# A hybrid diffusion step: the third modulation set of layers 1 to 3 summed on VectorE

## Chip, cores and metric

The kernel runs on one core of one Trainium2 chip. The metric is device time in microseconds (us); lower is better. The kernel before was timed three times, and one more execution of it was profiled; all stretches below are counted from the start of that execution's span.

## What is computed

One inference step through four layers on 384 tokens of width 1024 (128 context tokens, 256 latent tokens). Layer l mixes tokens by l mod 3: 0 is a bidirectional Mamba-2 scan (SSD), 1 a short gated convolution, 2 differential attention. So the order is SSD, short convolution, attention, SSD. Every layer then has a gated convolutional feed-forward net (FFN).

```python
mod = silu(cond) @ w_mod[l] + b_mod[l]            # cond: c_ctx for context tokens, c for latent ones
sh1, sc1, gt1, sh2, sc2, gt2 = split(mod, 6)      # six rows of 1024
m = mixer(rmsnorm(x, g[0]) * (1 + sc1) + sh1)
x = x + gt1 * rmsnorm(m, g[1])
f = ffn(rmsnorm(x, g[2]) * (1 + sc2) + sh2)       # (silu(gate) * val) @ w_down, after a 3-tap conv of h @ w_up
x = x + gt2 * rmsnorm(f, g[3])
```

The change concerns the first line: a product of two condition rows (context and latent) with a 1024 x 6144 float32 matrix per layer, 25 MB of weights.

## The kernel before

**Products.** Activations lie transposed, 128 channels on the partitions and 384 tokens along the free axis. All weights come as float32; each chunk of 128x1024 is loaded into `wr`, copied by ACT (ScalarE) to a rounded `wh` (line 155), and DVE (VectorE) writes the rest `wl = wr - wh` (line 156). A product is three matmuls, `wh*hh`, `wh*hl` and `wl*hh` (line 340 for channel-major results, line 380 for token-major ones, line 811 for the attention projections). `ahead` (line 143) keeps four chunks split (WS = 4) and three more loaded (WR = 4 buffers) ahead of the chunk that PE (TensorE) works on.

**Up products.** `ffn` (line 462) has 22 blocks. A block takes two chunks and two PSUM banks of five, 48 matmuls of 128x384. Then `conv` takes each of its two halves through one ACT copy (line 396) and four DVE operations (lines 398 and 400, two each), ACT does the SiLU (line 475) and DVE the product into `g[i]` (line 476). The down product follows in `tm_out`; its `prep` splits `g[k]` into `gh` and `gl` (lines 405 and 406).

**Modulation.** The 6144 columns of a layer are three sets s = 0, 1, 2 of 2048, and each set eight units, one for each block kb of 128 input channels. `mod_units` (line 167) makes for each unit a load of 1 MB (tag `wm` with one buffer, or `wx` with `room` buffers of the running stage's pool) and four float32 matmuls (line 187) of a stationary 128x32 (`sil`, the two condition columns and 30 zero columns) with 512 moving columns, placed in four column strips of the array, so that they can run beside each other. The profile shows each of the four as two instructions, so a unit is eight instructions of line 187. The eight units of a set add up in one PSUM bank; `mod_finish` (line 195) adds the bias row, multiplies by the norm weight (lines 197 and 198), turns the result with four PE transposes into `cm`, and writes the gates of sets 1 and 2 to memory (`gd`), from where `gates` broadcasts them. Set 0 is needed before a layer's mixer, set 1 at the end of the mixer, set 2 for the middle norm and the FFN's gate.

**Where the units run.** All 96 units stand in one list, `filler`. `pace` (line 242) takes units from it so that after each phase of a layer a given count is done: the numbers in `PACE` are the counts for the end of the mixer's products, the middle turn (mixer's out product and norm), the up products, and the end turn. Layer n = 0 does its own sets 1 and 2 in its mixer (16 units) and then 13 units of layer 1. A later mixer has 11 units: the last three of its set 1, and set 2. `need` takes units that are still missing when a set is used. `stock` loads ahead as many units as there are buffers.

**Order.** All loads are issued by one queue, SP's, in order. The order of instructions on each engine is made when the kernel is built: the framework keeps the program's order as a priority and lets later instructions go ahead on a simulated timeline where an engine would be idle. [...]

Of the kernel before, what the change touches and what calls it, by code (L numbers as in the profile page):

```python
# [10 lines left out]
F32 = mybir.dt.float32  # L11
# [8 lines left out]
P = 128  # L20
# [19 lines left out]
HB = 2  # L40
PACE = (24, 31, 32, 37)
CB = 9


class Net:
# [29 lines left out]
    def consts(self):  # L75
# [12 lines left out]
        self.V.memset(self.brow, 0.0)  # L88
        self.S.activation(self.sil, self.sil, AF.Silu)

    def consts2(self):
# [75 lines left out]
    def mod_units(self, l):  # L167
# [24 lines left out]

        return [(lambda s=s, kb=kb: load(s, kb), lambda raw, s=s, kb=kb: unit(s, kb, raw)) for s in range(3) for kb in range(KB)]

# [47 lines left out]
    def pace(self, phase, n, of):  # L242

        lo, hi = self.goal[phase]
        self.fill(lo + (hi - lo) * n // of - (24 * len(self.layers) - len(self.filler)))

# [104 lines left out]
    def tm_out(self, *args, room, **kw):  # L351

        with self.tc.tile_pool(name="out", bufs=1, reuse_waits="tile") as self.op:
            self.room, self.hbufs = room, HB
            self.stock()
            self._tm_out(*args, **kw)
            self.room = 0

    def _tm_out(self, l, gate, nk, prep, eps=None, then=None):
# [49 lines left out]
    def run(self):  # L409
# [6 lines left out]
        for l in self.layers:  # L416
            self.filler += self.mod_units(l)
        l0 = self.layers[0]
        with tc.tile_pool(name="in", bufs=1, reuse_waits="tile") as self.op, self.banked(mm=5):
# [14 lines left out]
        for n, l in enumerate(self.layers):  # L434
            nxt = self.layers[n + 1] if n + 1 < len(self.layers) else None
            marks = [8 if n == 0 else 24 * n + 16] + [24 * n + m for m in PACE]
            self.goal = dict(zip(("mix", "mid", "ffn", "end"), zip(marks, marks[1:])))
# [21 lines left out]
            with tc.tile_pool(name=f"ffn{l}", bufs=1, reuse_waits="tile") as pl, self.banked(mm=5):  # L459
                self.ffn(l, pl, end)  # L460

    def ffn(self, l, pl, then):
        d = self.d
# [3 lines left out]
        with self.tc.tile_pool(name=f"up{l}", bufs=1, reuse_waits="tile") as self.cpool:  # L467
            self.cbufs = 7
            for i in range(NF):
                ch = self.cm_weights(2)  # L470
                pg = self.cm_block(ch, 2, 0)
# [4 lines left out]
                self.V.tensor_tensor(g[i], tg, tv, op=ALU.mult)  # L476
                self.pace("ffn", i + 1, NF)

        def prep(k):
# [544 lines left out]
```

## Time and profile before

| | |
|---|---|
| median of 3 runs | 2422.38 us (2415.94 to 2424.57) |
| the profiled execution, own time | 2417.66 us |
| its span, first to last instruction | 2415.9 us |
| PE busy in the span | 2295.4 us (95%) |
| DVE busy | 1621.2 us (67%) |
| ACT busy | 1253.4 us (52%) |
| mean granted TensorE clock | 0.977 of full speed |
| moved by DMA | 391.79 MB |

The stages in the span: SSD mixer of layer 0 until about 448, its up products to 637, down products and end turn to 744; layer 1 (short convolution) to 912, up products to 1095, down to 1202; layer 2 (attention) to 1451, up products to 1637, down to 1745; layer 3 (SSD) to 2132, up products to 2317, down to the end. PE is matmul, PEld weight load, SPq SP's queue. A matmul's shown duration overlaps with the next one's, so what a matmul costs is read from the distance of the starts, and the sums of durations exceed the time. Releasers of waits are inferred.

### The profile page before, as it was taken

How to read it: one execution, taken by the hardware profiler on the slowest of the kernel's cores; microseconds unless marked ns; L12 is line 12 of the kernel's file. 1: busy time of each engine (PE TensorE's matmuls, PEld its weight loads, DVE VectorE, ACT ScalarE, POOL GpSimd, SP SyncE). 2: the span in 40 equal slices, each digit the busy share in tenths (PEclk: the TensorE clock that was granted, in tenths of full speed). 3: DMA queues.
4: the chain of work that ended last, by engine and by line, in shares of the span. 5: the costliest groups of instructions: out<-in, count | busy, mean ns of one | idle time of the engine just before them, and what ended most of it. 6: DMA issues, size and time to landing. Idle time of an engine off the chain costs nothing.

```text
span 2415.9 us, 35621 instructions
## 1 busy us (share of the span) xinstructions
PE 2295.4 (95%) x13132; PEld 2002.2 (83%) x13132; DVE 1621.2 (67%) x2930; ACT 1253.4 (52%) x2173; POOL 334.2 (14%) x498
## 2 busy tenths in 40 slices
PE   6989999899999999999999979999998999989998
PEld 3878887699987969998688649998687888779987
DVE  3787876577655457776655547776578888677765
ACT  3666765444444344444544444444556776554444
POOL 1122330100001010000123320000113323010000
PEclk7999999999999999999999999999999999989999
DMA  7556655533537564335435463335455654423442
GB/s 286 181 162 207 202 192 177 201 132 122 166 111 288 204 245 138 125 122 166 155 106 176 155 244 107 123 127 162 147 159 171 200 159 153 139 97 123 131 146 81
DMA packets 113374, 391.79 MB, mean 162 GB/s; under 512 B 13104, under 2 KB 25520, under 8 KB 100912
## 3 DMA queue, kind: packets, MB, share of 16 engines
q1 hardware_dynamic: 113200, 389.52, 49.2%
q8 instruction: 103, 1.69, 0.3%
q14 instruction: 71, 0.58, 0.1%
HBM read 382.39 MB, written 7.08 MB: 161 GB/s over the span
## 4 chain that ended last, share of the span: by engine, by line
PE 78%; DVE 9%; DMA 6%; ACT 3%; issue 2%; POOL 2%; SPq 0%; POOLq 0%; ACTq 0%; DVEq 0%
PE mm L340 44%; PE mm L380 20%; PE mm L811 4%; DMA wm<-in_w_mod 3%; PE modps L187 2%; PE yp L380 2%; DVE e L686 2%; DVE wl L156 1%; PE yp L726 1%; DVE w L690 1%; PE yp L852 1%; ACT jk L263 1%; DVE cv L398 1%; DMA wx<-in_w_mod 1%; PE yp L340 1%
## 5 line engine op out<-in xcount | busy, mean ns | idle before, releaser
L340 PE MATMUL mm<-hh,wh 128*128 128x384 f32 (+1 forms) x2352 | 796.4, 340 | 14.9 <-DVE cv L400 9.8
L340 PE MATMUL mm<-hl,wh 128*128 128x384 f32 (+1 forms) x2352 | 793.8, 338 | 0.0
L340 PE MATMUL mm<-hh,wl 128*128 128x384 f32 (+1 forms) x2352 | 792.0, 338 | 0.0
L156 DVE TENSOR_TENSOR wl<-wr,wh 128x1024 fp32r<-128x1024 f32 (+2 forms) x466 | 564.4, 1213 | 259.7 <-ACT wh L155 257.6
L155 ACT ACTIVATE wh<-wr 128x1024 fp32r<-128x1024 f32 (+2 forms) x466 | 483.3, 1039 | 313.1 <-PE mm L340 243.9
L340 PEld LDWEIGHTS mm<-hh,wh 128*128 128x128 f32 (+1 forms) x2352 | 443.3, 189 | 38.9 <-DVE cv L400 14.6
L340 PEld LDWEIGHTS mm<-hh,wl 128*128 128x128 f32 (+1 forms) x2352 | 442.3, 188 | 5.3 <-issue 3.4
L340 PEld LDWEIGHTS mm<-hl,wh 128*128 128x128 f32 (+1 forms) x2352 | 442.6, 188 | 4.5 <-issue 2.2
L396 ACT ACTIVATE cv<-mm,fcw 128x384 f32<-128x384 f32 x176 | 100.1, 571 | 233.4 <-PE mm L340 228.2
L380 PE MATMUL mm<-wh,gh 128*128 128x512 f32 x528 | 208.7, 395 | 0.0
L380 PE MATMUL mm<-wl,gh 128*128 128x512 f32 x528 | 208.6, 395 | 0.0
L380 PE MATMUL mm<-wh,gl 128*128 128x512 f32 x528 | 207.9, 395 | 0.0
L271 POOL TENSOR_SCALAR m<-s 128x1 f32<-128x1 f32 x42 | 17.2, 409 | 1145.5 <-ACT jk L263 1144.7
L398 DVE SCALAR_TENSOR_TENSOR cv<-mm,fcw,cv 128x127 f32<-128x127 f32 x352 | 144.1, 410 | 42.6 <-ACT cv L396 42.6
L405 ACT ACTIVATE gh<-fg 128x384 fp32r<-128x384 f32 x176 | 92.2, 524 | 152.6 <-PE mm L380 151.7
L406 DVE TENSOR_TENSOR gl<-fg,gh 128x384 fp32r<-128x384 f32 x176 | 97.6, 557 | 96.7 <-ACT gh L405 96.1
L400 DVE SCALAR_TENSOR_TENSOR cv<-mm,fcw,cv 128x127 f32<-128x127 f32 x352 | 145.8, 415 | 10.8
L380 PEld LDWEIGHTS mm<-wh,gh 128*128 128x128 f32 x528 | 99.0, 187 | 25.0 <-issue 0.8
L380 PEld LDWEIGHTS mm<-wh,gl 128*128 128x128 f32 x528 | 99.0, 187 | 24.2
L380 PEld LDWEIGHTS mm<-wl,gh 128*128 128x128 f32 x528 | 99.0, 187 | 23.9
L187 PE MATMUL modps<-wm,sil 128*32 128x512 f32 x496 | 78.3, 655 | 18.5 <-DMA wm<-in_w_mod 17.6
L683 POOL TENSOR_TENSOR w<-cb,dt 128x512 f32<-128x512 f32 x48 | 71.6, 1504 | 92.5 <-DVE w L691 91.6
(224 smaller groups left out, 3180.9 us busy)
## 6 DMA issues: line engine op xcount, KB each, us to landing
wr<-in_ffn_up SPq DMA_DIRECT2D x176, 512.0 KB
wm<-in_w_mod SPq DMA_DIRECT2D x62, 1024.0 KB
wr<-in_ssd_in SPq DMA_DIRECT2D x96, 512.0 KB
wr<-in_ffn_down SPq DMA_DIRECT2D x88, 512.0 KB
wx<-in_w_mod SPq DMA_DIRECT2D x34, 1024.0 KB
ab<-acs SPq DMA_DIRECT2D x48, 512.0 KB
wr<-in_ssd_out SPq DMA_DIRECT2D x32, 512.0 KB
wr<-in_sc_in SPq DMA_DIRECT2D x32, 384.0 KB
```

Of the source, the lines that this page charges most:

```text
L155: self.S.activation(hi[:, :m], raw[:, :m], AF.Copy)
L156: self.V.tensor_tensor(lo[:, :m], raw[:, :m], hi[:, :m].bitcast(F32), op=ALU.subtract)
L187: self.PE.matmul(acc[32 * j:32 * j + 32, :], self.sil[:, kb, :], raws[:, j // 2, (j % 2) * 512:(j % 2 + 1) * 512], start=kb == 0, stop=kb ...
L340: self.PE.matmul(acc[:m], w, h, start=n == 0, stop=n == len(ops) - 1)
L380: self.PE.matmul(acc[t], g[:, o:o + n], w, start=k == 0 and i == 0, stop=k == nk - 1 and i == 2)
L396: self.S.activation(t, src, AF.Copy, scale=cw[:, 1:2])
L398: self.V.scalar_tensor_tensor(t[:, o + 1:o + n], src[:, o:o + n - 1], cw[:, 0:1], t[:, o + 1:o + n], op0=ALU.mult, op1=ALU.add)
L400: self.V.scalar_tensor_tensor(t[:, o:o + n - 1], src[:, o + 1:o + n], cw[:, 2:3], t[:, o:o + n - 1], op0=ALU.mult, op1=ALU.add)
L405: self.S.activation(hi, src, AF.Copy)
L406: self.V.tensor_sub(lo, src, hi.bitcast(F32))
L683: GP.tensor_tensor(h4(w), cb[:, 1, t, None, :].to_broadcast([P, 4, P]), per(dt, 1), op=ALU.mult)
L811: PE.matmul(acc[t][:, :256], h[k][:, o:o + m], w[:, ws], start=k == 0 and i == 0, stop=k == KB - 1 and i == 2)
```

## The change

Sets 0 and 1 stay as they are, and so do all three sets of layer 0. Set 2 of layers 1, 2 and 3 leaves the list (`filler` has 24 + 3 x 16 = 72 units). It is computed beside the up products of the layer before. `mod_sums` goes through the eight channel blocks in halves of 1024 columns, 16 steps. A step loads 512 KB (`wv`, two buffers) and does two DVE operations on 128x1024, one for each condition row: `acc = raw * sil + acc`, with `sil` as a scalar on each partition. Sixteen of the 22 up blocks have such a step ahead of their own work (those with i mod 4 not 3, until the steps are used up). After the last block `mod_total` adds the 128 partitions on PE, with a stationary 128x32 that has ones in column c: four column strips for each of the two condition rows, eight matmuls, in the shape of two units. Then `mod_finish` runs as before.

`PACE` is moved by the eight units that each later layer lacks. `pace` also limits how many units `stock` loads ahead to those still due in the phase, and `tm_out` loads the next unit at its end, after its pool's room is set to 0.

```diff
-PACE = (24, 31, 32, 37)
+PACE = (0, 7, 8, 13)
...
+        self.onec = cp.tile([P, 2, 32], F32, name="onec")
+        self.V.memset(self.onec, 0.0)
+        for c in range(2):
+            self.V.memset(self.onec[:, c, c:c + 1], 1.0)
...
-        return [(lambda s=s, kb=kb: load(s, kb), lambda raw, s=s, kb=kb: unit(s, kb, raw)) for s in range(3) for kb in range(KB)]
+        sets = range(3 if l == self.layers[0] else 2)
+        return [(lambda s=s, kb=kb: load(s, kb), lambda raw, s=s, kb=kb: unit(s, kb, raw)) for s in sets for kb in range(KB)]
+
+    def mod_sums(self, l, s, pool):
+        acc = pool.tile([P, 2, 2048], F32, name="macc")
+        for kb in range(KB):
+            for hf in range(2):
+                raw = pool.tile([P, 1024], F32, tag="wv", name="wv", bufs=2)
+                self.load(raw, self.d["w_mod"][l, s, kb][:, hf])
+                for c in range(2):
+                    a, w = acc[:, c, hf * 1024:(hf + 1) * 1024], self.sil[:, kb, c:c + 1]
+                    if kb == 0:
+                        self.V.tensor_scalar(a, raw, w, None, op0=ALU.mult)
+                    else:
+                        self.V.scalar_tensor_tensor(a, raw, w, a, op0=ALU.mult, op1=ALU.add)
+                yield acc
+
+    def mod_total(self, l, s, acc):
+        res = self.modres[l]
+        ps = self.pm.tile([P, 512], F32, tag="mod", name="modps")
+        for j in range(4):
+            self.load(self.brow[32 * j:32 * j + 2], self.d["mrow"][l, s, j])
+        for c in range(2):
+            for j in range(4):
+                self.PE.matmul(ps[32 * j:32 * j + 32, :], self.onec[:, c, :], acc[:, c, 512 * j:512 * j + 512],
+                               start=c == 0, stop=c == 1, tile_position=(0, 32 * j))
+        self.mod_finish(l, s, ps, res, res["gd"])
...
     def pace(self, phase, n, of):
         lo, hi = self.goal[phase]
-        self.fill(lo + (hi - lo) * n // of - (24 * len(self.layers) - len(self.filler)))
+        done = lambda: self.units - len(self.filler)
+        for _ in range(lo + (hi - lo) * n // of - done()):
+            self.fill(1, max(1, hi - done()))
...
             self._tm_out(*args, **kw)
             self.room = 0
+        self.stock()
...
-            marks = [8 if n == 0 else 24 * n + 16] + [24 * n + m for m in PACE]
+            marks = [8 if n == 0 else 16 * n + 8 + PACE[-1]] + [16 * n + 24 + m for m in PACE]
...
-    def ffn(self, l, pl, then):
+    def ffn(self, l, pl, then, nxt):
...
+            acc = None
+            sums = self.mod_sums(nxt, 2, self.cpool) if nxt is not None else iter(())
             for i in range(NF):
+                if i % 4 != 3:
+                    acc = next(sums, acc)
                 ch = self.cm_weights(2)
...
                 self.pace("ffn", i + 1, NF)
+            if nxt is not None:
+                self.mod_total(nxt, 2, acc)
```

## Rows read from the trace of the kernel before

**Rows 1.** The page's first part: busy time of each engine.
```profile
PE 2295.4 (95%) x13132; PEld 2002.2 (83%) x13132; DVE 1621.2 (67%) x2930; ACT 1253.4 (52%) x2173; POOL 334.2 (14%) x498
```
**Rows 2.** The page's chain that ended last, by line.
```profile
PE mm L340 44%; PE mm L380 20%; PE mm L811 4%; DMA wm<-in_w_mod 3%; PE modps L187 2%; PE yp L380 2%; DVE e L686 2%; DVE wl L156 1%; PE yp L726 1%; DVE w L690 1%; PE yp L852 1%; ACT jk L263 1%; DVE cv L398 1%; DMA wx<-in_w_mod 1%; PE yp L340 1%
```
**Rows 3.** Busy time by stage; columns in the first line.
```profile
core 0: us, PE busy (x) PEld busy (x) DVE busy (x) ACT busy (x) POOL busy (x), PEclk, DMA share, GB/s
735.00:856.00 121.00, 116.24 (x681) 103.56 (x678) 59.81 (x104) 45.06 (x73) 3.98 (x5) 0.99 0.66 242
856.00:912.00 56.00, 50.90 (x265) 32.69 (x266) 32.32 (x47) 25.60 (x55) 11.57 (x20) 1.00 0.70 252
912.00:1095.00 183.00, 183.00 (x1057) 182.93 (x1057) 134.33 (x248) 80.36 (x116) 0.00 (x0) 1.00 0.38 124
1202.00:1358.00 156.00, 155.76 (x1143) 131.81 (x1144) 80.25 (x173) 72.53 (x189) 47.92 (x115) 1.00 0.44 142
1451.00:1637.00 186.00, 186.00 (x1061) 185.94 (x1061) 134.91 (x249) 83.08 (x120) 0.00 (x0) 0.99 0.37 120
```
**Rows 4.** DVE's groups in layer 1's up products (912 to 1095).
```profile
L156 DVE TENSOR_TENSOR wl<-wr,wh 128x1024 fp32r<-128x1024 f32 x43 | 52.7, 1226 | 33.9 <-ACT wh L155 33.9
...
L406 DVE TENSOR_TENSOR gl<-fg,gh 128x384 fp32r<-128x384 f32 x7 | 3.8, 549 | 0.0
```
**Rows 5.** Line 187 alone by stretch: PE busy, PEld busy, clock, DMA.
```profile
744.50:855.90 111.40, 9.67 (x76) 1.42 (x72) 1.00 0.65 238
...
880.00:912.00 32.00, 12.76 (x88) 2.48 (x88) 1.00 0.77 280
...
1187.00:1202.00 15.00, 4.92 (x32) 0.78 (x32) 0.82 0.64 245
...
1202.00:1358.00 156.00, 8.50 (x56) 1.23 (x56) 1.00 0.44 142
1358.00:1396.00 38.00, 3.20 (x24) 0.47 (x24) 0.96 0.47 161
...
1768.00:2050.00 282.00, 12.54 (x72) 1.72 (x72) 0.98 0.59 172
```
**Rows 6.** Timeline of PE in the short convolution, around one unit.
```profile
813.31 0.33 PE L340 MATMUL mm<-hl,wh 128*128 128x384 f32 x1
813.49 0.34 PE L340 MATMUL mm<-hh,wl 128*128 128x384 f32 x1
813.75 1.07 PE L187 MATMUL modps<-wm,sil 128*32 128x512 f32 x8
814.75 0.45 PE L340 MATMUL mm<-hh,wh 128*128 128x384 f32 x1
815.03 0.34 PE L340 MATMUL mm<-hl,wh 128*128 128x384 f32 x1
```
**Rows 7.** One SSD group of layer 3, busy by engine (columns as rows 3).
```profile
1916.29:1951.58 35.29, 34.49 (x231) 31.13 (x231) 30.11 (x61) 25.23 (x43) 10.81 (x11) 1.00 0.57 186
```
**Rows 8.** What PE waited for, 1745 to 1850: total us, times, longest.
```profile
PE modps L187 <- DMA wm<-in_w_mod: 3.3, 2, 2.0
```
**Rows 9.** Timeline of PE in layer 1's middle turn: two units in a row.
```profile
888.55 0.40 PE L380 MATMUL mm<-wl,sgh 128*128 128x512 f32 x1
888.79 0.40 PE L380 MATMUL mm<-wh,sgl 128*128 128x512 f32 x1
889.12 1.92 PE L187 MATMUL modps<-wx,sil 128*32 128x512 f32 x16
890.97 0.50 PE L380 MATMUL mm<-wh,sgh 128*128 128x512 f32 x1
891.31 0.40 PE L380 MATMUL mm<-wl,sgh 128*128 128x512 f32 x1
```
**Rows 10.** DVE's groups in the whole span, shapes apart.
```profile
L326 DVE SCALAR_TENSOR_TENSOR x<-rt,r,x 128x512 f32<-128x512 f32 x48 | 34.9, 767 | 5.9 <-POOL r L273 5.6
...
L312 DVE TENSOR_TENSOR hl<-h,hh 128x512 fp32r<-128x512 f32 x32 | 22.0, 688 | 0.7
...
L284 DVE TENSOR_SCALAR xn<-x,r 128x512 f32<-128x512 f32 x24 | 17.6, 735 | 20.1 <-POOL r L273 20.1
```
**Rows 11.** What SP's queue waited for in layer 2's up products.
```profile
SPq L63 <- DVE wl L156: 128.2, 22, 7.1
```
**Rows 12.** Layer 2's middle turn, busy by engine (columns as rows 3).
```profile
1411.00:1451.00 40.00, 28.47 (x153) 13.93 (x151) 21.89 (x36) 20.61 (x49) 13.53 (x20) 0.89 0.89 355
```

More of the change, by code (lines that the diff above doesn't have):

```diff
@@ L417, in run @@
             self.filler += self.mod_units(l)
+        self.units = len(self.filler)
         l0 = self.layers[0]
@@ L459, in run @@
             with tc.tile_pool(name=f"ffn{l}", bufs=1, reuse_waits="tile") as pl, self.banked(mm=5):
-                self.ffn(l, pl, end)
-    def ffn(self, l, pl, then):
+                self.ffn(l, pl, end, nxt)
+    def ffn(self, l, pl, then, nxt):
         d = self.d
```

## The prediction

> **What bounds the kernel now.** I read the page first. PE is busy 95% of the span, DVE 67%, ACT 52% [rows 1], and the chain of waits is mostly PE's three kinds of weight products, with line 187, the modulation units, at 2% and loads of `wm` at 3% [rows 2]. So PE is the engine to relieve. An average over stages does not say what a unit is worth in the stage that it leaves, nor what room DVE has in the stage that it goes to, so I went through the stages next.
>
> In the up products PE has no gap, at the full clock, and DVE is busy 134.33 of 183.00 us in layer 1 and 134.91 of 186.00 in layer 2 [rows 3]. DVE's idle time there is not lost work: 33.9 us of it ends with ACT's `wh` [rows 4], which waits for PE to give a buffer back. DVE walks behind PE and has about 49 us per layer free. The same rows show that the build puts later work into an engine's gaps: seven `gl` splits of the down product run inside the up products [rows 4]. The added work can use DVE's gaps in the same way, and it need not stand where the program has it.
>
> The mixers, which the units leave, are nearly full on PE too: 116.24 of 121.00 us in the short convolution, 155.76 of 156.00 in the attention's projections [rows 3], 34.49 of 35.29 in an SSD group [rows 7]. There a unit should cost its time.
>
> **What is removed.** 24 units, eight in each of three mixers. In the short convolution a unit stands alone between two blocks. From the last matmul before it to the second after it is 815.03 - 813.49 = 1.54 us; two ordinary steps are 2 x 0.175, so the unit delays PE by 1.19 us [rows 6]. Two in a row, by the same reckoning with steps of 0.235: 891.31 - 888.79 - 0.47 = 2.05, or 1.02 each [rows 9]. Attention's seven units in the projections are busy for 8.50 us, 1.21 each, and three more for 3.20, 1.07 each [rows 5]. The nine in layer 3's SSD are busy for 12.54, 1.39 each, some of them at a start that was slow anyway [rows 5]. A group has 0.80 us of PE idle for one unit, so a part may be hidden there. I take 8 x 1.19 = 9.5 for the short convolution, 8 x 1.1 = 8.8 for attention, 8 x 1.0 = 8.0 for SSD: **26.3 us**. The bounds are 24 x 0.2 = 5 (only what exceeds a gap of 0.8) and 24 x 1.39 = 33.
>
> The loads of these units go too, 1 MB each through a single `wm` buffer. In layer 3's start PE waits 3.3 us for two of them [rows 8]. Three units stay in that mixer and are spread wider, so I take 1 us off, between 0 and 3.3.
>
> At one point the Trainium skill speaks against this. "Perfetto Trace Analysis", section "Identifying the Most-Contended Engine", says that PE's matmul busy share is a poor measure of its headroom and names the weight-load share. By it the mixers would have room: 103.56 of 121.00 us, and 31.13 of 35.29 in the SSD group [rows 3, 7], so units would be worth little there. The delay of 1.19 us in the short convolution [rows 6] disagrees with that reading, at least there; it is the third rival below.
>
> **What is added on PE.** `mod_total` is eight matmuls of line 187's shape, two units in a row: 2.05 us [rows 9], three times: **+6.2 us**. It stands between up and down products, where PE is full, so I hide nothing of it. It waits for the last sum, made at block 20 of 0 to 21, so a block of 48 matmuls at 0.173 us (183.00 for 1057 [rows 3]), 8.3 us, lies between. The bias load, the four transposes and the gate writes of `mod_finish` come in either kernel, once for each set. If the sums were late, the down products' first matmuls, whose operands are early, could go ahead.
>
> **What is added on DVE.** 32 operations of 128x1024 per layer. No row has this operation at this size. In place, with a scalar per partition, at 128x512 it takes 767 ns; going from 512 to 1024 adds 1226 - 688 = 538 ns to the two-operand kind [rows 4, 10], so 1.305 us. Four of the 32 (block 0) have one tensor operand: 735 ns at 512, at most twice that [rows 10], say 1.0. Together 28 x 1.305 + 4 x 1.0 = 40.5 us. With layer 1's 134.3 that is 174.8 of 183: DVE is then 95% full, with 8.2 us to spare, and PE still sets the pace. Cost taken: **0**; above, if the room is not usable, 40.5 us for each layer.
>
> Is the room usable? Late DVE work hurts PE in two ways. A split chunk may be late: four are kept, so when PE hands one back it still has three, 3 x 24 x 0.173 = 12.5 us. Or a PSUM bank may be late: five banks of half a block each leave four halves, 16.6 us. One step is 2.6 us. Both margins cover it, provided the mean rate holds.
>
> **What moves in SP's queue.** Sixteen loads of 512 KB replace eight of 1 MB, with the same bytes. In layer 1's up products the rate goes from 124 to about 124 + 8.4 MB / 183 us = 170 GB/s, where another stretch shows 355 [rows 3, 12]. The queue waits mostly for `wr` buffers, 128.2 us in 22 waits, the longest 7.1 [rows 11]. A `wv` load behind such a wait comes up to 7.1 us late and takes 4.2 us at 124 GB/s; the sum, 11.3, is within the two blocks (16.6 us) that two buffers give. The other way round, a `wv` load that waits for its buffer holds the `wr` loads behind it, of which three chunks (12.5 us) are in store. Taken: 0.
>
> **The rest.** The limit on loading ahead shifts units between turns. Before, layer 1's middle turn ran eleven units and its end turn four [rows 5]; now it is seven or eight, and five. The number is the same; an end turn may wait once more for a 1 MB load, 3 us at 355 GB/s, in two layers. Taken 0, bound +6. The three memsets at the start are each below the 0.77 us of 128x512 [rows 10], and I cover them with the first loads: 0, bound +2.3.
>
> **The sum.** -26.3 - 1 + 6.2 = -21 us against the profiled execution's 2417.66 us, so 2396.6. Its time is 4.7 us below the median of the runs; against the median, 2422.38 - 21 = **2401 us**. The likeliest case's own range, from units at 1.0 to 1.25 and turns at 0 to +6, is 2392 to 2410. Half a per cent, 12 us, is about what a measurement of this kernel can tell from no change.
>
> **The rivals.**
>
> DVE becomes the bound (slower). Place: the up products of layers 0 to 2. Each step takes x us longer on DVE than I reckon, because the operation is dearer or because DVE stands at its head until `wv` has landed. 8.2 us per layer are free; PE's gain is 20.1 / 3 = 6.7 per layer. So the change breaks even at (8.2 + 6.7) / 16 = 0.93 us per step and is 0.5% slower at (8.2 + 6.7 + 4.0) / 16 = 1.18. At 2 us it would cost 3 x (32 - 8.2) = 71, a net +51: **2473 us**. For it: 95% is very full. Against it: the queue's margins above, and the rows of the operation at 512. Chance 0.10.
>
> The mixers do not get shorter by their units (no change). If SSD and attention are held by chains through DVE and ACT, where the units filled gaps, only the short convolution gains: -9.5 + 6.2 = -3, with a few us either way: **2419 us**. For it: DVE is busy 30.11 of 35.29 in the SSD group [rows 7], and the weight-load share above. Against it: PE's idle share there is 2%. With half of the gain in these two it is 2411. Chance 0.12.
>
> The clock falls (a smaller gain). Layer 1's middle turn ran with eleven units at 1.00; layer 2's, with PE idle 11.5 of 40 us, at 0.89, a mean between the two levels of 2.4 and 1.2 GHz [rows 3, 12]. If the first fell to 0.89, and the end turns lost as much again, 56 us x 0.11 = 6 and two turns of 15 us x 0.11 = 3 come back: about 2411. The Trainium skill ("TensorE: Matmul & The Clock Gate", section "Part 1: The HAM clock gate (the "warmup" mystery)") says that an idle PE falls to half its clock until it has been busy again; layer 2's row agrees. But the 24 units mostly leave mixers with hardly a gap. Chance 0.05.
>
> More than the units goes (larger gain). The single `wm` buffer's waits, and units that cost 1.39, end in full: -33 - 3.3 + 6.2 = -30, or 2392, and with the loads' 3% of the chain [rows 2] partly gone, down to 2380. Chance 0.08.
>
> **Chances and range.** The forecast has 0.65. Faster by over 0.5% (below 2410.3): 0.65 of the forecast, 0.08 of the larger gain and 0.03 from the clock's case: 0.76. Within 0.5%: 0.12, 0.02 and 0.02 of DVE's: 0.16. Slower: 0.08. The range goes from 2384 to 2424: it takes in the no-change case and most of the larger gain, and leaves out DVE's case and what lies under 2384, together about 0.15.
>
> **What would show it.** Line 187 in the short convolution's products at about three units instead of nine, and most of its blocks at 72 x 0.173 = 12.5 us from start to start instead of 12.5 + 1.19 = 13.7. Up products of layers 0 to 2 again at 183 to 189 us, without a wait of PE on `wl` or on line 400, and DVE at some 175 us in them. The new DVE operation near 1.3 us. SSD groups of layer 3 nearer 34.3 than 35.3. Wrong would be: up products over 190 us (DVE or its loads), groups still at 35.3 (gaps), or turns longer by more than 3 us each.

## The result and the profile after

The changed kernel takes **2473.52 us** (median of four runs, 2469.09 to 2476.81) where the kernel before takes 2419.83 (four runs, 2415.94 to 2424.57): a ratio of 1.022, 95% interval [1.0205, 1.0238]. It is slower by 54 us; forecast were 2401 us, between 2384 and 2424. The profiled execution has a span of 2474.6 us, 58.7 above that of before, and a mean granted clock of 0.962 (0.977 before).

The page of the kernel after first: busy time by engine, the chain that ended last by line, and two of the costliest groups.

```profile
PE 2309.0 (93%) x12988; PEld 2020.9 (82%) x12988; DVE 1713.1 (69%) x3029; ACT 1253.9 (51%) x2173; POOL 332.1 (13%) x498
...
PE mm L374 40%; PE mm L415 20%; PE mm L853 4%; DVE wl L160 2%; DVE e L728 2%; DVE macc L212 2%; PE modps L191 2%; PE yp L415 2%; DVE cv L433 1%; DMA wm<-in_w_mod 1%; PE yp L768 1%; PE yp L894 1%; DVE w L732 1%; DVE cv L435 1%; DMA wx<-in_w_mod 1%
...
L374 PE MATMUL mm<-hh,wh 128*128 128x384 f32 (+1 forms) x2352 | 805.0, 344 | 38.3 <-DVE cv L435 32.2
...
L212 DVE SCALAR_TENSOR_TENSOR macc<-wv,sil,macc 128x1024 f32<-128x1024 f32 x84 | 103.8, 1278 | 1.4 <-DMA wv<-in_w_mod 1.3
```

DVE's busy time rises only from 67% [rows 1] to 69%, and the new operation takes 1278 ns, not more than was reckoned. But line 212 now stands on the chain with 2%, and PE's largest group of weight products waits 38.3 us, 32.2 of it for line 435 (before: 14.9 and 9.8, for line 400, which is the same operation). Averages say that DVE has room; the chain says that it is late. So the time must be looked for by stage. (PE is busy for longer than before though it has 144 instructions fewer: part of them runs at a lower clock.)

The next table is worked out from the two traces: "up" reaches from the first start of PE's up products to one step (0.2 us) past the last, "down" from there to the first product of the next mixer (down products and end turn), "mix" from there to the next up products (mixer and middle turn); all in us.

```
          mix0   up0  down0  mix1   up1  down1  mix2   up2  down2  mix3   up3  down3   span
before   448.3 188.6 107.7  167.1 183.3 106.8  249.5 185.3 107.4  388.1 184.6  99.2  2415.9
after    448.2 199.1 107.7  165.8 201.3 108.4  254.8 200.6 112.0  392.2 185.6  98.9  2474.6
change    -0.1 +10.5   0.0   -1.3 +18.0  +1.6   +5.3 +15.3  +4.6   +4.1  +1.0  -0.3   +58.7
```

Two things stand there. The three up stages with the new sums lose 43.8 us, and the mixers gain nothing: -1.3, +5.3, +4.1. They hold 27 units less than before, 10, 10 and 7: the 24 that were taken out, and three that now run in other stages.

**The up products.** Two halves of layer 1's up products in the kernel after, busy by engine (columns as in rows 3), and DVE's group of the sums in the first half:

```profile
core 0: us, PE busy (x) PEld busy (x) DVE busy (x) ACT busy (x) POOL busy (x), PEclk, DMA share, GB/s
921.00:1010.00 89.00, 82.03 (x435) 76.66 (x435) 82.57 (x128) 31.63 (x46) 0.00 (x0) 0.93 0.58 190
1010.00:1122.00 112.00, 112.00 (x648) 112.00 (x647) 83.47 (x155) 48.99 (x69) 0.00 (x0) 1.00 0.40 132
```

```profile
L212 DVE SCALAR_TENSOR_TENSOR macc<-wv,sil,macc 128x1024 f32<-128x1024 f32 x28 | 34.6, 1277 | 0.7 <-DMA wv<-in_w_mod 0.7
```

All 28 accumulations of the layer stand in the first half, none in the second. In the first half DVE is busy 93% and PE idles 7.0 us at a clock of 0.93; in the second DVE has 28.5 us free and PE runs without a gap. Over the whole stage DVE's busy time is 166.0 us, even below the 174.8 that was forecast: the room was there, and the work was not put into it. The chain of waits of the same stage:

```profile
921.19 27.13 PE mm L374 x144
...
957.71 0.96 DVE macc L212
958.67 0.40 DVE cv L435
959.32 2.39 DVE macc L212 x2
...
979.84 0.40 DVE cv L435
980.24 2.39 DVE macc L212 x2
...
997.14 0.98 PE modps L223 x4
...
1002.51 1.84 PE modps L223 x12
...
1008.72 1.00 PE modps L191 x8
1009.72 112.55 PE mm L374 x648
```

Between 957 and 987 the chain runs over DVE again and again: the sums (line 212) stand ahead of the conv's operation on line 435, which must read a PSUM bank before PE can write it again. From 1009.72 on PE runs 648 matmuls in one piece, as before. The layer's 18.0 us are then accounted for: 7.0 of idle, 0.03 of 201 us = 6.0 of clock, 0.98 + 1.84 = 2.8 of `mod_total` and 1.0 for one unit make 16.8. The 2.8 us are layer 1's; in all three stages together PE also waits 2.8 us for the last sums ahead of `mod_total` (line 223), the longest time 2.4, in layer 2's.

**The mixers.** The chain in the short convolution's products of the kernel after:

```profile
755.10 14.27 PE mm L374 x72
...
784.07 12.71 PE mm L374 x72
...
797.22 0.97 PE modps L191 x2
...
810.89 1.83 PE modps L191 x10
...
839.93 1.83 PE modps L191 x10
```

The units have not left the products. The units' line alone, in the products and in the middle turn, first before and then after (columns as in rows 5; the first count of each row takes in matmuls that only reach into the stretch, the weight loads count exactly):

```profile
744.60:855.90 111.30, 9.57 (x76) 1.42 (x72) 1.00 0.66 238
855.90:911.70 55.80, 12.80 (x92) 2.48 (x88) 1.00 0.70 251
755.00:870.80 115.80, 12.78 (x76) 2.37 (x72) 0.98 0.56 191
870.80:920.80 50.00, 1.09 (x11) 0.16 (x8) 0.88 0.47 169
```

The products have nine units in either kernel; the ten units that are gone left the middle turn (eleven before, one after). There they had covered PE's waits: after, PE waits 8.6 us in this turn for `xn`, the norm's output, where before no wait for `xn` stands in it. PE's transposes waiting for `xn` in all that follows layer 0's mixer, before and after (total us, times, longest):

```profile
PE tp L294 <- DVE xn L284: 14.8, 4, 4.4
PE tp L328 <- DVE xn L318: 31.7, 6, 7.2
```

What is more, the units in the products now mostly come ten instructions at a time, one unit and a quarter of another, and take 1.83 us where eight take 1.00. With that, and with a first block that takes 14.27 us instead of 12.70, at a clock of 0.88, the products need 115.8 us (111.3 before); the turn needs 50.0 (55.8 before), at a clock of 0.88.

In layer 3's SSD the group's period did not fall to 34.3; it stayed or rose. Groups of the kernel after by engine, and the chain's piece of 24 matmuls at the head of each group:

```profile
2006.54:2043.41 36.87, 35.07 (x223) 32.55 (x224) 28.40 (x60) 24.63 (x42) 11.39 (x11) 0.95 0.46 139
2043.41:2078.70 35.29, 33.49 (x223) 30.97 (x223) 28.40 (x60) 23.60 (x39) 11.28 (x11) 1.00 0.50 145
```

```profile
1969.66 6.02 PE mm L374 x24
...
2006.54 6.01 PE mm L374 x24
...
2043.41 4.44 PE mm L374 x24
...
2078.70 6.01 PE mm L374 x24
```

The hole in such a group before, with its unit, at the end of rows 7 (start, duration, instruction; in brackets PE's idle time before it):

```profile
1949.72 1.07 PE L187 MATMUL modps<-wm,sil 128*32 128x512 f32 x8
1951.58 0.45 PE L340 MATMUL mm<-hh,wh 128*128 128x384 f32 x1 [0.80 <-DVE cv L400]
```

With a unit in its hole the group took 35.29 us [rows 7]. Without it PE has eight instructions less and idles 1.80 us there instead of 0.80, and the group takes 35.29 at the full clock: the unit had cost nothing. Where the clock falls, it takes 36.87, and the 24 matmuls after the hole 6.02 instead of 4.44.

### The profile page after: what moved, and what is told of

It reads as the page before. It is cut to its first block, busy times and chain, and to the rows that moved or that the text cites. A ratio compares the mean times of both kernels' runs of the same rounds, so it can differ in the third digit from the quotient of the medians.

```text
span 2474.6 us, 35476 instructions
## 1 busy us (share of the span) xinstructions
PE 2309.0 (93%) x12988; PEld 2020.9 (82%) x12988; DVE 1713.1 (69%) x3029; ACT 1253.9 (51%) x2173; POOL 332.1 (13%) x498
## 4 chain that ended last, share of the span: by engine, by line
PE 74%; DVE 14%; DMA 4%; ACT 3%; issue 3%; POOL 2%; SPq 0%; POOLq 0%; DVEq 0%; ACTq 0%
PE mm L374 40%; PE mm L415 20%; PE mm L853 4%; DVE wl L160 2%; DVE e L728 2%; DVE macc L212 2%; PE modps L191 2%; PE yp L415 2%; DVE cv L433 1%; DMA wm<-in_w_mod 1%; PE yp L768 1%; PE yp L894 1%; DVE w L732 1%; DVE cv L435 1%; DMA wx<-in_w_mod 1%
## 5 line engine op out<-in xcount | busy, mean ns | idle before, releaser
L374 PE MATMUL mm<-hh,wh 128*128 128x384 f32 (+1 forms) x2352 | 805.0, 344 | 38.3 <-DVE cv L435 32.2
L433 DVE SCALAR_TENSOR_TENSOR cv<-mm,fcw,cv 128x127 f32<-128x127 f32 (+1 forms) x352 | 143.4, 410 | 39.8 <-ACT cv L431 39.8
L435 DVE SCALAR_TENSOR_TENSOR cv<-mm,fcw,cv 128x127 f32<-128x127 f32 (+1 forms) x352 | 144.6, 414 | 7.9
L212 DVE SCALAR_TENSOR_TENSOR macc<-wv,sil,macc 128x1024 f32<-128x1024 f32 x84 | 103.8, 1278 | 1.4 <-DMA wv<-in_w_mod 1.3
```

Source lines behind the costliest of these rows:

```text
L212: self.V.scalar_tensor_tensor(a, raw, w, a, op0=ALU.mult, op1=ALU.add)
L374: self.PE.matmul(acc[:m], w, h, start=n == 0, stop=n == len(ops) - 1)
L433: self.V.scalar_tensor_tensor(t[:, o + 1:o + n], src[:, o:o + n - 1], cw[:, 0:1], t[:, o + 1:o + n], op0=ALU.mult, op1=ALU.add)
L435: self.V.scalar_tensor_tensor(t[:, o:o + n - 1], src[:, o + 1:o + n], cw[:, 2:3], t[:, o:o + n - 1], op0=ALU.mult, op1=ALU.add)
```

## The experiments

Each run is compared with the kernel before on the same chip. The diffs of e1 to e3 are against the changed kernel, those of e4, e5, e7, e8 and e12 against e1, that of e6 against e3, those of e9 to e11 against the kernel before; only their core is shown. In the table stages are worked out as above; "idle" is PE's idle time from layer 0's up products to the end, and "clock" the sum over the same stages of length times (1 - granted clock), both as differences to before (73.1 and 32.3 us). Where PE idles at the low clock the two overlap, and the clock is shown to 0.01, so a sum is good to some 5 us. Taken from the traces' unrounded clock and over PE's busy time alone, so that nothing is counted twice, the clock's difference is +25.5 in the kernel after, +18.9 in e1, +17.1 in e3, +10.4 in e9 and +15.5 in e10.

```
                         ratio    span    up0   up1   up2   mix1  mix2  mix3   idle  clock
before                          2415.9  188.6 183.3 185.3  167.1 249.5 388.1
after                    1.0222 2474.6  199.1 201.3 200.6  165.8 254.8 392.2  +43.5  +32.3
e1_paced                 1.0099 2442.9  183.2 184.8 184.8  164.6 257.4 394.7  +21.3  +26.5
e2_few_sums              1.0107 2441.2  183.3 184.8 185.2  164.6 256.9 396.2  +18.2  +31.2
e3_no_sums_96_units      1.0103 2440.8  183.4 183.2 183.2  171.6 267.6 388.6   +6.9  +19.7
e4_layer1_paced          1.0102 2437.7  183.4 184.8 185.5  164.7 262.3 389.7   +9.4  +17.4
e5_paced_free_ahead      1.0076 2434.9  193.6 185.9 184.6  163.9 253.2 389.0  +16.6  +27.1
e6_96_units_mid10        1.0071 2434.9  183.3 185.5 185.3  170.4 260.5 387.1   +3.6   +9.8
e7_paced_pe_cover        1.0110 2444.6  183.2 185.2 184.8  165.7 261.5 391.5   +9.4  +25.6
e8_paced_own_bank_mid10  1.0064 2429.8  183.2 183.2 185.9  165.7 255.3 388.5  +15.1  +24.3
e9_before_18_units_out   0.9967 2405.8  188.2 183.2 183.2  160.8 247.9 388.8   +3.8   +6.2
e10_before_end_36        1.0086 2440.3  188.2 183.3 185.2  169.9 265.5 392.7   +5.4  +17.0
e11_before_mid_30        1.0004 2419.8  183.3 183.2 184.8  168.9 252.2 387.2   -2.5   +6.6
e12_atomic_units         1.0900 2632.8  184.1 184.4 183.1  201.7 291.4 394.8 +100.8  +81.8
```

**e1_paced: the same sums, spread over the stage.** The scalar of each sum passes through a GpSimd operation that also reads the first column of the FFN block before. So the build cannot put a step ahead of the block that it belongs to.

```diff
+                    if self.key is not None:
+                        k = pool.tile([P, 1], F32, tag="key", name="key", bufs=4)
+                        self.GP.tensor_scalar(k, self.key, 0.0, w, op0=ALU.mult, op1=ALU.add)
+                        w = k
...
                 if i % 4 != 3:
+                    self.key = g[i - 1][:, 0:1] if i >= 1 else None
```

> The changed kernel, with each step of the sums tied to the block before it: its scalar operand goes through a small GpSimd operation that also reads the block's product, so that step i cannot run before block i-1 is done. Same work otherwise. Theory A (the build puts the 16 steps in the first 80 us of the up products, ahead of the convolutions, where DVE has no room; spread over 21 blocks they fit): the three up stages return from 200 to 183-189 us, the total to 2424-2434. Theory B (95% of DVE is too full however it is spread): up stages stay above 195, total above 2455.

Measured: 2442.19 us beside 2417.48, ratio 1.0099 [1.0079, 1.0120]. The first half of layer 0's up products in the kernel after, and then both halves in e1 (columns as in rows 3):

```profile
448.00:530.00 82.00, 74.80 (x420) 70.00 (x417) 75.49 (x114) 31.65 (x44) 0.00 (x0) 1.00 0.65 219
...
```

```profile
450.40:532.00 81.60, 81.60 (x471) 81.60 (x472) 70.22 (x124) 37.90 (x55) 3.51 (x14) 1.00 0.57 185
532.00:633.60 101.60, 101.60 (x591) 101.35 (x591) 91.25 (x152) 45.09 (x63) 4.04 (x16) 1.00 0.50 163
```

The same 32 operations, spread, cost the up stages nothing: 183.2, 184.8 and 184.8 us, PE without a gap, as the prediction had it, with DVE 88% full. That the sums were bunched is so shown to be the cause of the up stages' loss (`mod_total` now stands behind the up products, in "down"), and e1 gives back 31.7 us of span. But the whole is still 1% slower than before, above theory A's 2424 to 2434. Of the 27.0 us that are left, 12.0 lie in the three mixers and 16.1 in the down products with their end turns, which take 116.2, 107.2 and 114.6 us for 107.7, 106.8 and 107.4.

**e2_few_sums: hardly any sums.** Of the 32 DVE operations of a layer 28 are left out (the four of block 0 stay); loads and `mod_total` stay.

```diff
-                for c in range(2):
+                for c in range(2 if kb == 0 else 0):
```

> The changed kernel with the sums of channel block 0 alone: 28 of the 32 DVE operations per layer are left out, the 16 loads and the partition add stay. Whatever the up stages lost to DVE comes back: 184-188 us each, total about 2428. Then what is left against the kernel before is the mixers' and turns' doing. If the units had been worth 1.0 to 1.2 us each in the mixers, as I predicted, the total would be 2400; theory C (the units sat in holes of PE, and without them the holes stay and the clock falls) says 2420-2432. If the loads or the partition add cost the up stages something, these stay above 190.

Measured: 2444.24, ratio 1.0107 [1.0086, 1.0129], and every stage within 2 us of e1. The total is above all that was expected, theory C's 2432 included. What remains has nothing to do with the sums on DVE.

**e3_no_sums_96_units: none of the move.** All 96 units stay on PE, with the counts of before; only the two other edits stay, the limit on loading ahead and the `stock` at the end of a turn. (`own(l)` in the diffs of e3 and e6 is the number of units that layer l has in the list.)

```diff
+SUMS = ()
...
-        sets = range(3 if l == self.layers[0] else 2)
+        sets = range(2 if l in SUMS else 3)
...
-            sums = self.mod_sums(nxt, 2, self.cpool) if nxt is not None else iter(())
+            sums = self.mod_sums(nxt, 2, self.cpool) if nxt in SUMS else iter(())
```

> No layer uses the sums: all 96 units run on PE as before, but with the changed limit on loading ahead and the extra load at the end of a turn. Theory C (the missing units did it): within 8 us of before, 2412-2428. Rival D (the limit on loading ahead and the early load alone disturb mixers and turns): 2428 or more.

Measured: 2442.36, ratio 1.0103 [1.0079, 1.0128]. With the work of before unchanged, the kernel is 25 us slower, as rival D had it: mix1 +4.5, mix2 +18.1, mix0 +1.8, the other stages together even. The instruction orders that the build makes tell the two edits apart: with the limit alone PE's order is that of e3; without it, with `stock` or not, it is that of before. So the limit costs this, by the order that the build makes of the same units. Idle +6.9 and clock +19.7 make up for it, within the 5 us: the trace has +23.1 from layer 0's up products on, and with the clock over busy time alone the two make +24.0.

An obvious rival is that the units' loads come late. It isn't borne out here: from layer 0's up products on PE waits 16.1 us for them in the kernel before, 16.1 in e1 and 12.2 in e3. In e10, further down, it is 23.0, but also 19.9 in e11, which loses nothing.

**e4_layer1_paced: the move for layer 1 alone,** spread as in e1, layers 2 and 3 with 24 units each, and the limit.

```diff
+SUMS = (1,)
```

> Only layer 1's third set is summed on DVE, paced as in the first run; layers 2 and 3 have their units on PE. The short convolution is the mixer with the fewest gaps. As predicted (units at 1.19 us, 2.05 us for the partition add, up stage unchanged): 7 us below before. Theory C for the turns alone: the middle turn loses its cover and the gain is 0 to 4 us.

Measured: 2439.82, ratio 1.0102 [1.0077, 1.0127]: mix1 164.7 as in e1, mix2 and mix3 between e1's and e3's; neither of the two expected gains is there. One layer or three, the loss is the same, which speaks for an order that is worse as a whole and against a price per moved set.

**e5_paced_free_ahead: spread sums, no limit.** The limit can only go if `mod_total` does not need the one PSUM bank and the one `brow` that units ahead of it may hold, so it gets its own.

```diff
-        ps = self.pm.tile([P, 512], F32, tag="mod", name="modps")
+        ps = self.psum()
+        rows = self.cpool.tile([P, 2, 512], F32, name="brow2")
...
-            self.fill(1, max(1, hi - done()))
+            self.fill(1)
```

> The paced sums of the first run, with loading ahead as free as in the kernel before. For that the partition add gets a PSUM bank and bias rows of its own (else it needs those of set 1, which free loading ahead starts earlier, and the order can't be planned). If the limit on loading ahead costs what the third run showed (25 us), and the 24 units were worth what I predicted, the total is 2397-2402. Theory C (the units sat in holes) says 2412-2424: the limit's cost is gone, the units gain nothing. If the limit is not the cause in this kernel, it stays at 2435-2445.

Measured: 2436.71, ratio 1.0076 [1.0061, 1.0091]. Better than e1 by 5.5 us, no more; by what was expected, the limit is then not what makes this kernel slow, or not by itself. Without the limit another order results (up0 193.6, mix2 253.2), which isn't that of before either.

**e6_96_units_mid10: e3 with later counts** for the middle turns.

```diff
-            marks = [8 if n == 0 else past + (16 if own(l) == 24 else 13)] + [past + own(l) + m for m in PACE]
+            marks = [8 if n == 0 else past + (16 if own(l) == 24 else 13)] + [past + own(l) + m for m in (PACE if n == 0 else (0, 10, 11, 13))]
```

> All 96 units on PE and the limit on loading ahead, as in the third run, but from layer 1 on the counts ask for ten units in the middle turn instead of seven, as many as free loading ahead let run there. If the limit costs because of where the units run (fewer in the middle turn's gaps, more in the end turn and the next mixer), the total returns to 2415-2427. If the order of the loads itself is what costs, it stays at 2435 or more.

Measured: 2435.68, ratio 1.0071 [1.0056, 1.0086]. Again all the work of before, and 18 us slower than it: the middle turns' share of the units alone isn't what costs. The expectation puts 2435 and more down to the order of the loads; the run doesn't show that, and the waits for the units' loads, 19.4 us for 16.1 before, are too small for it.

**e7_paced_pe_cover: e1 with unread matmuls in the holes,** eight of 128x128 in each of layer 3's eight scan groups, and eight behind each of the three groups of the last heads' transposes in attention. Nothing reads their results.

```diff
+                if l == 3 and src is Bc:
+                    for _ in range(8):
+                        PE.matmul(tr[:, 3, :], self.ident, src[:, 0:P], start=True, stop=True)
...
+                for _ in range(8 if n == 3 else 0):
+                    PE.matmul(tr[:, 2, :], self.ident, on[:, 0, :], start=True, stop=True)
```

> The first run with idle work for PE: eight 128x128 matmuls whose results nobody reads, behind the first transposes of each scan group of layer 3, and as many behind the last heads of the attention; some 12 us of PE work in all. Theory C's clock part (after a hole of 1.8 us the granted clock falls and 24 matmuls take 6.0 instead of 4.4 us): layer 3's mixer gets shorter by 3 to 10 us in spite of the added work, the total falls to 2430-2440. Rival (PE's time is what counts there): both get longer, 2448 or more.

Measured: 2445.54, ratio 1.0110 [1.0093, 1.0127]. The chain's pieces of 24 matmuls in layer 3, first two of e1's and then e7's:

```profile
1937.27 6.02 PE mm L378 x24
...
1974.15 4.43 PE mm L378 x24
```

```profile
1943.73 4.44 PE mm L378 x24
...
1979.02 4.43 PE mm L378 x24
...
2014.32 4.43 PE mm L378 x24
...
2049.61 4.44 PE mm L378 x24
```

In layer 3 PE does 64 matmuls more and the mixer takes 391.5 us instead of 394.7; its idle time falls from 36.9 to 23.1 us, and the slow pieces are gone. In SSD's groups the clock's fall is so shown to come from the empty hole. In attention the same means made the mixer longer (261.5 for 257.4), so the run as a whole shows no gain.

**e8_paced_own_bank_mid10: e1 with its own bank and e6's counts.**

```diff
-        ps = self.pm.tile([P, 512], F32, tag="mod", name="modps")
+        ps = self.psum()
...
-            marks = [8 if n == 0 else 16 * n + 8 + PACE[-1]] + [16 * n + 24 + m for m in PACE]
+            marks = [8 if n == 0 else 16 * n + 8 + PACE[-1]] + [16 * n + 24 + m for m in (PACE if n == 0 else (0, 10, 11, 13))]
```

> Paced sums with the bank and rows of their own, the limit on loading ahead, and ten units in the middle turns from layer 1 on. Between the fifth and the first run if the place of the units matters: 2415-2430; at 2440 if it does not.

Measured: 2433.46, ratio 1.0064 [1.0048, 1.0081], the best with the sums on DVE, and between its two expectations. Against e6, with the same counts and limit and all 96 units, mix1 is shorter by 4.7 us, mix2 by 5.2 and mix3 longer by 1.4: 8.5 us for the 23 units that these mixers hold less. (The bank is another too.)

**e9_before_18_units_out: what units are worth in the kernel before.** It leaves out the matmuls of 18 of the 24 units (set 2 of layers 1 to 3, kb 1 to 6); their loads stay.

```diff
-            for j in range(4):
+            for j in range(0 if s == 2 and l != self.layers[0] and 0 < kb < KB - 1 else 4):
```

> The kernel before, with the matmuls of 18 of the 24 units left out (set 2 of layers 1 to 3, all but the first and the last block of channels); their loads stay, no sums, no partition add, loading ahead as it was. It measures what PE's work of these units is worth where it stood. My prediction's 1.1 us each: 20 us less, 2398. Theory C (they sat in holes): less than 10 us, 2408 to 2420.

Measured: 2410.99 beside 2420.79, ratio 0.9967 [0.9950, 0.9984]; the span is shorter by 10.1. Six units each left mix1 (-6.3 us), mix2 (-1.6) and mix3 (+0.7). The chain in layer 3's SSD groups, as above:

```profile
1902.73 4.43 PE mm L340 x24
...
1938.02 6.02 PE mm L340 x24
...
1974.89 6.02 PE mm L340 x24
...
2011.77 4.43 PE mm L340 x24
```

At 1.1 us a unit, an estimate from rows 5 and 9, PE did lose 18 x 1.1 = 19.8 us of work. 3.8 came back as idle time and 6.2 as clock, which leaves -9.8; the trace has -8.7 over the same stages (with the clock over busy time alone the sum is -5.6). By layer the signs come out, the sizes only to some 3 us: in mix1 -6.6 of work, -2.3 of idle, +1.6 of clock, -7.3 against -6.3 measured; in mix2 -6.6 + 2.7 + 2.4 = -1.5 against -1.6; in mix3 -6.6 + 4.6 + 4.0 = +2.0 against +0.7. This is the removal without any sums, limit or new counts, and about half of it is gone.

**e10_before_end_36 and e11_before_mid_30: the kernel before with one unit per layer moved,** from the end turn to the next mixer (e10), from the middle turn to the end turn (e11). No work is added or removed.

```diff
-PACE = (24, 31, 32, 37)
+PACE = (24, 31, 32, 36)
```

```diff
-PACE = (24, 31, 32, 37)
+PACE = (24, 30, 31, 37)
```

> Control: the kernel before with one unit per layer moved from the end turn to the next mixer (the last count 36 instead of 37). No work is added or taken. If mixers and turns depend little on where units stand, it stays within 4 us of before. If the planned order decides (a theory for what is left of the limit's cost), attention's tail and the turns move by 5 us or more.

> Control: the kernel before with one unit per layer moved from the middle turn past the up products (counts 30, 31 instead of 31, 32). As in the control before: within 4 us, or 5 us and more if the planned order decides.

Measured: e10 2442.34, ratio 1.0086 [1.0071, 1.0101]; e11 2420.36, ratio 1.0004 [0.9992, 1.0015]. One unit per layer, moved to another place in the list, costs 22 us in one case and nothing in the other. The unit's own place doesn't explain it: most of e10's loss is in attention's mixer (+16.0), which has 22 units in either kernel, and there in the stage of the last heads (52.9 us before, 64.9 in e10), with three units in either. What the count changes is the order that the build makes of the other work as well: with the units left aside, PE's order of lines and tiles in e10's trace differs from before at 761 of 12364 places, and in e11's at 1551. Two windows of this stage by engine, first the kernel before and then e10 (columns as in rows 3):

```profile
1380.00:1390.00 10.00, 7.40 (x28) 3.56 (x26) 7.02 (x16) 5.61 (x19) 5.81 (x18) 1.00 0.27 108
1390.00:1400.00 10.00, 10.00 (x43) 7.86 (x43) 3.50 (x9) 3.31 (x11) 2.50 (x8) 0.83 0.09 35
```

```profile
1395.00:1405.00 10.00, 6.52 (x23) 3.69 (x24) 6.11 (x14) 5.73 (x19) 5.02 (x15) 0.90 0.01 4
1405.00:1415.00 10.00, 10.00 (x31) 6.71 (x30) 3.31 (x8) 3.31 (x11) 2.24 (x8) 0.59 0.14 51
```

After a window in which PE idles 3.5 of 10 us comes one in which it is busy 10.00 of 10.00 and gets 31 matmuls done instead of 43, at a clock of 0.59 instead of 0.83, near the lower of the two levels (1.2 of 2.4 GHz). In the whole stage e10 has 7.9 us of idle for 5.0, and a clock of 0.87 over 64.9 us for 0.97 over 52.9, which is 8.4 us for 1.6. 2.9 + 6.8 are 9.7 of the 12.0. That the order sets the time is so shown; why this order leaves longer holes is not.

**e12_atomic_units: e8 with the four matmuls of a unit held together,** so that the build cannot cut a unit in two as in the short convolution.

```diff
-            for j in range(4):
-                self.PE.matmul(acc[32 * j:32 * j + 32, :], self.sil[:, kb, :],
+            with self.tc.tile_critical():
+                for j in range(4):
+                    self.PE.matmul(acc[32 * j:32 * j + 32, :], self.sil[:, kb, :],
```

> The eighth run with the four matmuls of a unit planned as one piece, so that no unit is cut in two. In the short convolution of the changed kernel a pause of 1.9 us between blocks held ten instructions of line 191 where eight take 1.07. If cut units cost there, the short convolution's stage falls by 3 to 6 us and the total to 2424-2430; if not, it stays at 2430-2436.

Measured: 2640.02, ratio 1.0900 [1.0882, 1.0918]. Already layer 0's mixer takes 94 us more than before. The means is far worse than the harm, and what the cut units cost remains untested; why it is so much worse isn't shown.

No version here beats the kernel before with all of its work in it.

## Why the prediction was wrong

The measured time is all but that of the rival "DVE becomes the bound" (2473). The place was that rival's; its mechanism was not. It asked for steps dearer by 2 us; each was as cheap as forecast (2 x 1.278 us for 2 x 1.305, 0.749 for 1.0), DVE's busy time was below the forecast, and spread steps (e1) cost nothing. Besides, only some 44 of the 58.7 us lie in the up stages. The number agrees by chance. The prediction's own sign, up products over 190 us, did point at the right stages.

**"The added work can use DVE's gaps in the same way, and it need not stand where the program has it": the step that failed first.** It took the build's freedom to put work early as a help. Rows 4 showed splits that run ahead into gaps, and the same freedom let 16 steps, whose operands depend on nothing but a load, run as fast as DVE and the `wv` loads allowed. The margins of 12.5 and 16.6 us were reckoned for one late step of 2.6 us; they met a row of steps, with DVE at 93% over 89 us. "Provided the mean rate holds" stood in the text, and a mean over the stage was used for it. Cost taken 0; found 10.5, 18.0 and 15.3 us in the three stages, 2.8 of layer 1's 18.0 being `mod_total`.

**"The rest": mis-sized.** The limit was taken at 0, bound +6. Alone, with all units on PE (e3), it costs 25 us. In the kernel with the sums that price isn't shown: there e5, without the limit, gives back 5.5 us. The step looked at how many units change place and at what a load may wait, and not at what the build makes of another place. e10 prices that: 22 us for a count that is lower by one, where e11 pays nothing for a like change. The durations of units don't give this price. What an order costs shows as idle and clock (e3: +6.9 and +19.7; e10: +5.4 and +17.0). Why just this order leaves longer holes in attention's last heads remains open.

**"What is removed", 26.3 us: right as work of PE, wrong as time.** Units cost PE about 1 us (eight instructions take 1.00 on the chain of the short convolution, where e9's six cost 111.3 - 105.9 = 5.4 us, 0.9 each). Three things took the gain. First, in SSD a unit filled a hole ahead of a wait for line 400: the rival "the mixers do not get shorter by their units" was right there, and in attention mostly (e9: +0.7 and -1.6 us for six units each). Second, the empty hole lowers the clock, 6.02 for 4.44 us. Third, in the short convolution the units that left were those of the middle turn, where they had covered the norm's waits; the forecast had the products at three units instead of nine, and they kept nine. It took the counts in the list for places, while the build puts a unit where it finds its slot.

Two readings in this part were off without deciding it. The 116.24 of 121.00 us for the short convolution start 9.6 us before its products; in these PE is busy for all of 111.30. And units at 1.25 us give a lower end of 2422.4 - 30 - 1 + 6.2 = 2398 us, not 2392.

The weight-load share that the prediction cited from the Trainium skill ("Perfetto Trace Analysis", section "Identifying the Most-Contended Engine") spoke for that rival, and for SSD the runs agree with it: with PE's matmuls busy 34.49 of 35.29 us and its weight loads 31.13 [rows 7], or 88%, a unit was worth nothing. It doesn't tell the mixers apart: in the short convolution's products, from 744.6 to 855.9, weight loads are busy 101.47 of 111.30 us, 91%, and a unit was worth 0.9 us. What differs is PE's gap ahead of a wait, 0.80 us in the SSD group and none in these products.

**"The clock falls": mechanism right, place and size wrong.** It was looked for in the turns, at 9 us. In e1, where the up stages are whole, the account is -26.3 + 6.2 of work, +21.3 of idle and +26.5 of clock, together +27.7, where the trace has +25.0 over the same stages. For the kernel after it is -20.1 + 43.5 + 32.3 = +55.7, where the trace has +58.8. With the clock over busy time alone the sums are +20.1 and +48.9, so 5 and 10 us stay without a name; units that are cut in two are a candidate. The Trainium skill ("TensorE: Matmul & The Clock Gate", section "Part 1: The HAM clock gate (the "warmup" mystery)") says that an idle PE falls to half its clock until it has been busy again; e7 agrees, where matmuls that nobody reads shorten layer 3's mixer by 3.2 us.

**What held.** `mod_total`, nearly: 2.82 us on layer 1's chain for 2.05 (forecast 6.2 for three; between e6 and e8 the three "down" stages grow by 2.6, 0.7 and 2.7). In the kernel after it ran inside the up products, not behind them. The loads of the units: PE's waits for `wm` in layer 3's start went from 3.3 to 2.4 us, for 1 us taken off. The loads in SP's queue: DVE waited for `wv` 1.3 us ahead of line 212 in the whole kernel, and 8.7 in three waits ahead of the first steps (line 210), at the head of the stages. DVE's price per step.

## What to carry to other kernels

Work that depends on nothing but a load has no place of its own under a build that fills gaps: it runs in one piece at the head of its stage, so reckon the engine's load over that piece, or tie each step to the block that it shall run beside. Before work is taken off an engine, look at what follows the slot that it leaves: work that sat in a hole gives nothing back, and the empty hole may lower the clock of what comes next. Price an edit of the order by a control in which the order alone changes; here one count lower by one, with the same work, cost 22 us, as much as the whole move was to bring.

## What the runs showed of the hardware

Behind a hole of 1.80 us in dense work the clock fell, in three of the four groups shown. The timeline of PE in the kernel after, at the head of an SSD group, where before had a unit (columns: start, duration, instruction; in brackets the idle time before it):

```profile
1964.55 0.34 PE L374 MATMUL mm<-hl,wh 128*128 128x384 f32 x1
1964.72 0.33 PE L374 MATMUL mm<-hh,wl 128*128 128x384 f32 x1
...
1969.66 0.44 PE L374 MATMUL mm<-hh,wh 128*128 128x384 f32 x1 [1.80 <-DVE cv L435]
...
1970.65 0.53 PE L374 MATMUL mm<-hl,wh 128*128 128x384 f32 x1
1970.97 0.53 PE L374 MATMUL mm<-hh,wl 128*128 128x384 f32 x1
```

The granted clock in the same stretch (columns as in rows 3):

```profile
1971.00:1973.00 2.00, 2.00 (x8) 2.00 (x7) 2.00 (x4) 1.99 (x3) 0.22 (x1) 0.50 0.80 164
```

The distance of the starts is 0.17 us before the hole, still so for the first matmuls behind it, and 0.32 soon after: the full clock and then the lower of the two levels, 1.2 of 2.4 GHz. The fall costs 1.6 us for 24 matmuls, nearly as much as the hole itself. It does not come each time: of the four groups shown of the kernel after one takes 4.44. In the kernel before, with 0.80 us in the same place, the pieces take 4.43 to 4.46. With eight matmuls of 128x128 in each hole (e7) all four take 4.43 or 4.44.

A modulation unit cut in two is dear. Eight instructions in four column strips take 1.00 us together, ten take 1.83 and two alone 0.97 (the chain of the short convolution): one strip alone costs as much as all four beside each other. What that adds up to over the kernel isn't shown (e12).
